# First attention slot leaves PSUM unscaled, and the loads of x for its mean square are spread over the passes

## The chip, the core and the metric

The kernel runs on one core of a Trainium2 chip. Its engines are TensorE (PE, with its weight loads shown apart as PEld), VectorE (DVE), ScalarE (ACT), GpSimd (POOL) and SyncE (SP, which here only issues DMAs). The metric is the device time of one execution in microseconds; lower is better.

## The reference, cut to what matters

One layer of an encoder with 256 tokens and width 2048, in float32:

```python
h = rms_norm(x, norm1_g)               # x * rsqrt(mean(x^2) + eps) * g
proj = h @ w_in                        # z | xBC | dt | q | k | v | GLU | gates
y_ssd = ssd_mixer(..., dt, ...) @ w_ssd_o
y_att = dilated_attention_mixer(q, k, v, q_g, k_g) @ w_attn_o
...
q = rms_norm(q.reshape(shape), q_g)    # per head, 128 wide
k = rms_norm(k.reshape(shape), k_g)
```

The factor `rsqrt(mean(x^2) + eps)` is one number for each token, called r below. Since it is a factor of the whole row, `h @ W` is `r * ((x * g) @ W)`. The kernel uses this for its first columns: it multiplies `x * g` with the weights of dt, q, k and v of the first head slot before r is known, and applies r to the results.

## The kernel before, in words

**Units.** All weights are streamed from HBM once. A weight block is a set of up to 512 output columns; it is cut into units of 256 rows of the weight (2 rows of 128 partitions). The main loop makes one pass for each unit, `for k in range(NU)`: it issues the weight load of unit k+5 on SP (five buffers `raw`), splits unit k+3 into a high and a low part (`split`: `hi` by ACT at L1211, `lo` by DVE at L255, four buffers each), issues the matmuls of unit k on PE (`mm`: L1273, L1274 and L1276 where activations are stationary, L1264, L1266 and L1268 where weights are), and then calls `S.tick`. So `hi` of unit k+3 can only be written when the matmuls of unit k-1 have read their `hi`, and `lo` when they have read their `lo`. "Unit k" and "pass k" below mean this number.

**Blocks at the start.** Units 0 to 7 are dt and q of slot 0 (448 columns), 8 to 15 k of slot 0 (384 columns), 16 to 23 v of slot 0 (384 columns). All three take `xgh`/`xgl`, the split of `x * g`. Units 24 to 31 are the first GLU block (512 columns); it and most later blocks take `hh`/`hl`, the split of the normed h. `job_h` makes these in four groups of four 128-row parts: four DVE products `hf` (L354), one ACT copy `hh` (L357), one DVE difference `hl` (L255, before the next group's `hl` but behind the next group's `hf` and `hh` in the code). Unit 24 needs group 0, unit 26 group 1, unit 28 group 2, unit 30 group 3. Two PSUM tiles `main` take turns, so block n+2 needs `main` of block n read.

**The planner.** What is to be done beside the stream is written as generators (jobs). A job yields requests: `("a", n)` or `("v", n)` asks to issue work that is costed at n ns on ACT or DVE, `"p"` on PE, `("m", n)` asks for n slabs of SBUF, `("b", n)` for banks of PSUM, `("w", n)` waits until n more passes have begun their tick, `("j", f)` waits until f is true. `S.tick` gives each engine credit: in a pass of 384 columns ACT gets (2600 - 950) * 0.75 * 0.95 = 1176 and DVE 1040, in a pass of 512 columns 1568 and 1387; credit left over is cut at 1.2 gains (1411 and 1248 for 384 columns). A request is granted while the credit is above zero, and may take it below zero. Jobs are asked in order of priority (0 first), then of age. All of this happens while the program is built: it sets the order in which each engine's instructions are issued.

**Forcing.** Before unit 24 is issued, `S.require` wants `hl` of group 0 to have been issued. If it isn't, it forces jobs without regard to credit or waits: first all jobs of priority 0 as far as they go, then those of priority 1 in order of age, until the condition is true. The same holds at units 26, 28 and 30.

**Jobs around the change.** `job_rms1` (priority 0, started in pass 3) loads x by four DMAs (`xr`, L318), squares it on ACT with a running sum (L325), makes r by ACT sqrt (L270) and five small DVE operations (`rstd_steps`, L273 to L283), stores it as `st["r1"]`, and calls `spread`: DVE makes a diagonal of r (`dg`, L291), PE multiplies it with ones (L296), and DVE copies the result to `rbc` (L338), which `job_h` (priority 1) waits for. `job_dt` (priority 1) multiplies dt's columns with r (L386) and permutes them on PE (L395). `job_qk` (priority 0) squares q or k from PSUM (L459), waits for r, makes the per-head factors by a second `rstd_steps`, multiplies them with r (L482), writes the normed `qn` from PSUM (L489), transposes it on PE (L501), and copies it out (L505, L506). `job_v` (priority 0) copies v out of PSUM times r (L517). `job_att` (priority 2) does the attention of the slot.

Of the kernel before, what the change touches and what calls it, by code (L numbers as in the profile page):

```python
# [15 lines left out]
AF = mybir.ActivationFunctionType  # L16
ALU = mybir.AluOpType
# [173 lines left out]
def kernel(ctx: ExitStack, tc: tile.TileContext, xT, xn, par, cm, cd, cq, w1, wq, ws, out):  # L191
    nc = tc.nc
    S = Sched()
# [11 lines left out]
    def nm(s):  # L205
        cnt[0] += 1
        return f"{s}_{cnt[0]}"

    def slab(shape, dt=F32, name="s"):
        return gp.tile([P] + list(shape), dt, tag="g", name=nm(name))  # L210

    def bank(shape=(512,), name="b"):
        return pd.tile([P] + list(shape), F32, tag="d", name=nm(name))

    def small(shape, name, dt=F32, bufs=None):
        return sm.tile([P] + list(shape), dt, tag=name, name=nm(name), bufs=bufs)

    V, A, G, PE = nc.vector, nc.scalar, nc.gpsimd, nc.tensor
# [11 lines left out]
    def par_(k, i=0, n=1):  # L230
        o = _OFF[k][0] + i
        return cpar[:, o:o + n]
# [11 lines left out]
    st = {}  # L244


    def natural(ap):

        return ap.rearrange("p (j r) -> p r j", r=2)

    def strided(ap):
        return ap.rearrange("p (r j) -> p r j", r=2)
# [29 lines left out]
            yield "v", 200 + n  # L282
        V.tensor_tensor(dst, r, s, op=ALU.mult)  # L283

    def spread(r):

        yield "m", 1
        dg = slab([2, P], name="dg")
        yield "v", 400
        for t in range(2):  # L290
            V.tensor_scalar(dg[:, t, :], ID, r[:, t:t + 1], None, op0=ALU.mult)  # L291
        yield "w", 1
        yield "b", 1
        b = bank()
        yield "p", 440
        PE.matmul(b[:, :T], ones, dg, start=True, stop=True)  # L296
        S.give()
        yield "w", 1
        return b[:, :T]
# [10 lines left out]
    def job_rms1():  # L310

        xss = small([2, 2], "xss1", bufs=1)
        yield "m", 4
        xs_ = []
        for t in range(2):
            for e in range(2):
                xr = slab([1024], name="xr")
                nc.sync.dma_start(xr, xn.rearrange("(p t) d -> p t d", t=2)[:, t, e * 1024:e * 1024 + 1024])  # L318
                xs_.append(xr)
        yield "w", 2  # L320
        for t in range(2):
            for e in range(2):
                yield "a", 1300
                xr = xs_[2 * t + e]
                A.activation(xr, xr, AF.Square, accum_out=xss[:, t, e:e + 1])  # L325
        S.give(4)
        yield "w", 1
        m2 = small([2], "ms2", bufs=2)
        yield "v", 300
        V.tensor_reduce(m2, xss, axis=AX.X, op=ALU.add)  # L330
        V.tensor_scalar(m2, m2, 1.0 / D, EPS, op0=ALU.mult, op1=ALU.add)
        r2 = cp.tile([P, 2], F32, name="r2")
        yield from rstd_steps(r2, m2, 2)
        st["r1"] = r2
        b = yield from spread(r2)
        rbc = small([T], "rbc", bufs=1)
        yield "v", 400
        V.tensor_copy(natural(rbc), strided(b))  # L338
        S.banks += 1
        st["rbc1"] = rbc  # L340
# [27 lines left out]
    def job_dt(main):  # L368
        bias = par_("dtb", 0, 64)
        yield "m", 2  # L370
        tmp = slab([8, P], name="dtt")
        pm_ = slab([2, T], name="perm")
        nc.scalar.dma_start(pm_, cq)
        dv, e, z, z2, q = (tmp[:, i, :] for i in range(5))
        raw = tmp[:, 5:7, :].rearrange("p a b -> p (a b)")
        dt = cp.tile([P, 2, 64], F32, name="dt")
        adt = cp.tile([P, 2, 64], F32, name="adt")
        adh = cp.tile([P, 2, 64], F32R, name="adh")
        adl = cp.tile([P, 2, 64], F32, name="adl")
        ea = cp.tile([P, 64], F32, name="ea")  # L380
        sp = cp.tile([P, 4, HEADS], F32, name="sp")
        st.update(dt=dt, adh=adh, adl=adl, sp=sp)
        yield "j", lambda: "r1" in st
        yield "v", 400
        for t in range(2):
            V.tensor_scalar(raw[:, 64 * t:64 * t + 64], main[:, t, 0:64], st["r1"][:, t:t + 1], None, op0=ALU.mult)  # L386
        V.memset(raw[:, P:P + 64], 0.0)
        st["dt_read"] = True
        yield "w", 1
        yield "b", 1  # L390
        ps = bank((2, P))
        yield "p", 900
        for t in range(2):
            for k in range(2):
                PE.matmul(ps[:, t, :], pm_[:, k, t * P:t * P + P], raw[:, 64 * k:64 * k + P],  # L395
                          start=(k == 0), stop=(k == 1))
        yield "w", 1
        yield "v", 300
        V.tensor_tensor(dv.rearrange("p (a b) -> p a b", a=2), ps[:, :, 0:64], bias[:, None, :].to_broadcast([P, 2, 64]),
                        op=ALU.add)  # L400
        S.banks += 1
        yield "a", 1900
        A.activation(e, dv, AF.Abs)
        A.activation(e, e, AF.Exp, scale=-1.0)
        A.activation(ea, par_("alog", 0, 64), AF.Exp)
        yield "w", 1
        yield "v", 1500
        V.tensor_scalar(z2, e, 2.0, None, op0=ALU.add)
        V.reciprocal(z, z2)
        V.tensor_tensor(z, z, e, op=ALU.mult)  # L410
        V.tensor_tensor(z2, z, z, op=ALU.mult)
        yield "v", 1000
        V.tensor_scalar(q, z2, 1.0 / 19.0, None, op0=ALU.mult)
        for n in (8, 7, 6, 5):
            V.scalar_tensor_tensor(q, q, 1.0 / (2 * n + 1), z2, op0=ALU.add, op1=ALU.mult)
        yield "v", 1000
        for n in (4, 3, 2, 1):
            V.scalar_tensor_tensor(q, q, 1.0 / (2 * n + 1), z2, op0=ALU.add, op1=ALU.mult)
        yield "v", 1000
        V.scalar_tensor_tensor(q, q, 1.0, z, op0=ALU.add, op1=ALU.mult)  # L420
        V.tensor_scalar(q, q, 2.0, None, op0=ALU.mult)
        V.scalar_tensor_tensor(dt.rearrange("p a b -> p (a b)"), dv, 0.0, q, op0=ALU.max, op1=ALU.add)
        for t in range(2):
            V.scalar_tensor_tensor(adt[:, t, :], dt[:, t, :], -1.0, ea, op0=ALU.mult, op1=ALU.mult)
        S.give(2)
        yield "w", 1
        yield "a", 200
        A.activation(adh, adt, AF.Copy)
        yield "w", 1
        yield "v", 200  # L430
        V.tensor_tensor(adl, adt, adh.bitcast(F32), op=ALU.subtract)
        yield "b", 1
        ps = bank((4, P))
        yield "p", 900
        for i, m in enumerate((GT, LE, LT, GE)):
            PE.matmul(ps[:, i, :], m, adt.rearrange("p a b -> p (a b)"), start=True, stop=True)
        yield "w", 1
        yield "a", 1500
        for i, o in enumerate((0, 64, 96, 32)):
            A.activation(sp[:, i, :], ps[:, i, o:o + HEADS], AF.Exp)  # L440
        S.banks += 1
        yield "w", 1
        yield "v", 300
        V.tensor_tensor(sp[:, 0, :], sp[:, 0, :], dt[:, 0, 0:32], op=ALU.mult)
        V.tensor_tensor(sp[:, 2, :], sp[:, 2, :], dt[:, 1, 32:64], op=ALU.mult)
        st["dt_done"] = True
# [3 lines left out]

    def job_qk(main, off, key, gain, scaled=False):

        yield "w", 1
        ss = small([6], "ss", bufs=3)
        junk = small([P], "junk", bufs=1)
# [7 lines left out]
        if scaled:  # L463
# [3 lines left out]
            r = st["r1"]  # L467
# [3 lines left out]
            for t in range(2):  # L471
                V.tensor_scalar(ms[:, t * 3:t * 3 + 3], ss[:, t * 3:t * 3 + 3], rr[:, t:t + 1], EPS,
                                op0=ALU.mult, op1=ALU.add)
# [12 lines left out]
        for t in range(2):  # L486
            for i in range(3):
                yield "a", 280
                A.activation(qn[:, t, i, :], main[:, t, off + i * P:off + i * P + P], AF.Copy,  # L489
                             scale=rs[:, t * 3 + i:t * 3 + i + 1])  # L490
        if off:
            yield "j", lambda: "dt_read" in st
        st["main_free"].add(id(main))
        st["q_blocks"] += 1
        yield "w", 3 if scaled else 1
        yield "b", 2
        bs = [bank((2, T)), bank((2, T))]
        yield "p", 650
# [11 lines left out]
    def job_v(main, j):  # L510
        yield "m", 1
        v = slab([2, 384], name="v")
        yield "j", lambda: j > 0 or "r1" in st
        yield "w", 1
        for t in range(2):
            yield "a", 450
            A.activation(v[:, t, :], main[:, t, 0:384], AF.Copy, scale=1.0 if j else st["r1"][:, t:t + 1])  # L517
        st["main_free"].add(id(main))
        st["q_blocks"] += 1
        qkv["v", j] = v  # L520


# [544 lines left out]
    def job_down(main, r, i):  # L1067
# [8 lines left out]
        for t in range(2):  # L1076
# [7 lines left out]
              main_free=set(), conv_t=set(), q_blocks=0, att_n=0, ssd_c=[0] * 4, ssd_n=0, z_n=0, z_g=[False] * 4, mg_n=0,  # L1084
# [16 lines left out]
    def start_jobs():  # L1101
        S.add(job_rms1(), "rms1", 0)
# [298 lines left out]
```

## Time and profile before

| | us |
|---|---|
| median of 3 runs (1982.23 to 1984.48) | 1983.19 |
| the profiled execution's own time | 1983.86 |
| its span, first to last instruction | 1982.1 |
| PE busy | 1966.0 (99%) |
| DVE busy | 1309.0 (66%) |
| ACT busy | 1036.0 (52%) |
| HBM read | 360.45 MB, 183 GB/s over the span |
| mean granted TensorE clock | 0.999 |

PE is busy nearly the whole span, and the chain that ended last is PE for 95% of it. So the profile is read by what is left: the few places where PE waits, and the one where its clock is low, are all in the first 100 us.

### The profile page before, as it was taken

The numbers are of one execution on the slowest core, as the hardware profiler recorded it, in microseconds if no ns is written. First come the engines' busy times: TensorE is split into PE (matmuls) and PEld (weight loads), VectorE is DVE, ScalarE is ACT, GpSimd is POOL, SyncE is SP. The second block draws the span as 40 slices with busy tenths as digits, with TensorE's granted clock in tenths as the row PEclk, the third lists the DMA queues.
The fourth block names the chain that finished last, engine by engine and source line by source line (L and its number), as shares of the span: only waits on it lengthen the run. The fifth ranks groups of instructions, "written<-read, shape, count | busy, mean of one in ns | idle before, by whom it ended". The sixth has DMA issues, their size and how long they took to land.

```text
span 1982.1 us, 29949 instructions
## 1 busy us (share of the span) xinstructions
PE 1966.0 (99%) x11798; PEld 1766.0 (89%) x11798; DVE 1309.0 (66%) x1847; ACT 1036.0 (52%) x1446; POOL 47.5 (2%) x42
## 2 busy tenths in 40 slices
PE   8999999999999999999999999999999999999999
PEld 7999999999998888888888888999988998998887
DVE  5778887887887889896654555555555554455443
ACT  6654576777757655545654444544443443344332
POOL 0000010000000000003000000000000000000000
PEclk9999999999999999999999999999999999999999
DMA  8555554554554555555555556555555555555554
GB/s 284 184 175 183 165 185 145 167 172 144 184 170 161 176 181 178 183 191 187 190 191 183 189 189 207 194 186 192 188 190 189 189 191 191 188 186 191 190 181 149
DMA packets 105342, 364.51 MB, mean 184 GB/s; under 512 B 11760, under 2 KB 12272, under 8 KB 105200
## 3 DMA queue, kind: packets, MB, share of 16 engines
q1 hardware_dynamic: 103904, 360.23, 55.4%
q10 hardware_dynamic: 1296, 2.36, 0.3%
q8 instruction: 92, 1.51, 0.3%
q14 instruction: 50, 0.41, 0.1%
HBM read 360.45 MB, written 2.10 MB: 183 GB/s over the span
## 4 chain that ended last, share of the span: by engine, by line
PE 95%; DVE 0%; issue 0%
PE main L1273 19%; PE main L1274 19%; PE main L1276 19%; PE main L1266 11%; PE main L1264 11%; PE main L1268 11%; PE b L842 1%; PE b L864 1%; PE b L968 1%; PE b L1273 0%; PE b L1274 0%; PE b L1276 0%; PE b L819 0%; PE b L501 0%; PE b L757 0%; PE b L742 0%
## 5 line engine op out<-in xcount | busy, mean ns | idle before, releaser
L255 DVE TENSOR_TENSOR lo<-raw,hi 128x1024 fp32r<-128x1024 f32 (+2 forms) x697 | 831.5, 1194 | 643.5 <-ACT hi L1211 638.7
L1211 ACT ACTIVATE hi<-raw 128x1024 fp32r<-128x1024 f32 (+2 forms) x695 | 716.2, 1032 | 868.7 <-PE main L1274 487.8
L1273 PE MATMUL main<-hi,hh 128*128 128x512 f32 (+1 forms) x800 | 306.1, 383 | 0.0
L1274 PE MATMUL main<-hi,hl 128*128 128x512 f32 (+1 forms) x800 | 299.0, 374 | 0.0
L1266 PE MATMUL main<-x2l,hi 128*128 128x256 f32 x1024 | 246.4, 281 | 0.0
L1264 PE MATMUL main<-x2h,hi 128*128 128x256 f32 x1024 | 246.3, 279 | 0.0
L1266 PE MATMUL main<-hl,hi 128*128 128x256 f32 x896 | 216.3, 281 | 3.2 <-DVE hl L255 3.2
L1264 PE MATMUL main<-hh,hi 128*128 128x256 f32 x896 | 217.7, 282 | 0.0
L565 DVE SCALAR_TENSOR_TENSOR co<-cin,cpar,co 128x256 f32<-128x256 f32 x480 | 211.1, 491 | 0.0
L1276 PE MATMUL main<-lo,hh 128*128 128x512 f32 (+1 forms) x800 | 200.5, 372 | 0.0
L1264 PEld LDWEIGHTS main<-x2h,hi 128*128 128x128 f32 x1024 | 192.7, 188 | 0.2
L1266 PEld LDWEIGHTS main<-x2l,hi 128*128 128x128 f32 x1024 | 192.6, 188 | 0.2
L1273 PE MATMUL main<-hi,ah 128*128 128x512 f32 x480 | 188.9, 394 | 0.0
L1274 PE MATMUL main<-hi,al 128*128 128x512 f32 x480 | 188.6, 393 | 0.0
L1273 PEld LDWEIGHTS main<-hi,hh 128*128 128x128 f32 x800 | 152.5, 191 | 23.4 <-ACT hi L1211 1.2
L1274 PEld LDWEIGHTS main<-hi,hl 128*128 128x128 f32 x800 | 152.2, 190 | 22.9 <-issue 1.9
L1266 PEld LDWEIGHTS main<-hl,hi 128*128 128x128 f32 x896 | 168.8, 188 | 4.2 <-DVE hl L255 3.6
L1264 PEld LDWEIGHTS main<-hh,hi 128*128 128x128 f32 x896 | 169.2, 189 | 0.6
L1276 PEld LDWEIGHTS main<-lo,hh 128*128 128x128 f32 x800 | 148.0, 190 | 22.1
L1268 PE MATMUL main<-x2h,lo 128*128 128x256 f32 x1024 | 138.3, 277 | 0.0
L1276 PE MATMUL main<-lo,ah 128*128 128x512 f32 x480 | 130.1, 393 | 0.0
L1268 PEld LDWEIGHTS main<-x2h,lo 128*128 128x128 f32 x1024 | 127.6, 188 | 0.0
(244 smaller groups left out, 2304.5 us busy)
## 6 DMA issues: line engine op xcount, KB each, us to landing
raw<-ws_dram SPq DMA_DIRECT2D x600, 512.0 KB, 3.3
raw<-wq_dram SPq DMA_DIRECT2D x88, 384.0 KB, 3.1
raw<-w_dram SPq DMA_DIRECT2D x7, 448.0 KB, 7.0
xr<-xn_dram SPq DMA_DIRECT2D x4, 512.0 KB, 9.2
x<-xn_dram SPq DMA_DIRECT2D x4, 512.0 KB, 4.3
xt<-xT_dram SPq DMA_DIRECT2D x7, 256.0 KB, 7.0
out_dram<-x SPq DMA_DIRECT2D x4, 256.0 KB, 3.7
out_dram<-x ACTq DMA_DIRECT2D x4, 256.0 KB, 5.6
```

Source lines behind the costliest of these rows:

```text
L255: V.tensor_tensor(lo, raw, hi.bitcast(F32), op=ALU.subtract)
L565: V.scalar_tensor_tensor(dst[:, e, :], x[:, e, k:k + T], par_("dw", (2 * i + e) * 31 + k), dst[:, e, :], op0=ALU.mult, op1=ALU.add)
L842: PE.matmul(ba, lt, src, start=(n == 0), stop=(n == 3))
L864: PE.matmul(bd[:, i, :], em[:, 0, i, :], x[:, c, pr:pr + P], start=True, stop=True)
L968: PE.transpose(b[:, e, t * P:t * P + P], src[:, t, k * P:k * P + P], ID)
L1211: A.activation(h, r, AF.Copy)
L1264: PE.matmul(o, wh[:, e, cs], ah, start=(first and e == 0 and c % 2 == 0), stop=False, skip_group_check=True)
L1266: PE.matmul(o, wh[:, e, cs], al, start=False, stop=False, skip_group_check=True)
L1268: PE.matmul(o, wl[:, e, cs], ah, start=False, stop=(last and e == 1), skip_group_check=True)
L1273: PE.matmul(o, ah[:, xs_], wh[:, e, :], start=(first and e == 0), stop=False)
L1274: PE.matmul(o, al[:, xs_], wh[:, e, :], start=False, stop=False)
L1276: PE.matmul(o, ah[:, xs_], wl[:, e, :], start=False, stop=(last and e == 1))
```

## The change

The four loads of `xr` are issued two passes apart instead of together. q, k and v of the first slot are copied from PSUM to SBUF as they are (`qraw`, and `v` in place), which frees `main` at once; r is applied to the copies. dt's columns are read from q's copy. `spread` waits two passes instead of one before its matmul, and q's and k's transposes come one pass after `qn` instead of three.

```diff
-    def spread(r):
+    def spread(r, wait=1):
...
-        yield "w", 1
+        yield "w", wait
         yield "b", 1
...
                 xr = slab([1024], name="xr")
                 nc.sync.dma_start(xr, xn.rearrange("(p t) d -> p t d", t=2)[:, t, e * 1024:e * 1024 + 1024])
                 xs_.append(xr)
-        yield "w", 2
+                yield "w", 2
+        yield "w", 1
...
-        b = yield from spread(r2)
+        b = yield from spread(r2, 2)
...
-        yield "j", lambda: "r1" in st
+        yield "j", lambda: "r1" in st and "dt_raw" in st
+        yield "w", 1
         yield "v", 400
         for t in range(2):
-            V.tensor_scalar(raw[:, 64 * t:64 * t + 64], main[:, t, 0:64], st["r1"][:, t:t + 1], None, op0=ALU.mult)
+            V.tensor_scalar(raw[:, 64 * t:64 * t + 64], st["dt_raw"][:, t, 0:64], st["r1"][:, t:t + 1], None, op0=ALU.mult)
...
     def job_qk(main, off, key, gain, scaled=False):
 
+        if scaled:
+            yield "m", 1
+            raw = slab([2, 448], name="qraw")
+            yield "w", 1
+            for t in range(2):
+                yield "a", 500
+                A.activation(raw[:, t, :off + 384], main[:, t, :off + 384], AF.Copy)
+            st["main_free"].add(id(main))
+            st["q_blocks"] += 1
+            main = raw
+            if off:
+                st["dt_raw"] = raw
...
-        if off:
-            yield "j", lambda: "dt_read" in st
-        st["main_free"].add(id(main))
-        st["q_blocks"] += 1
-        yield "w", 3 if scaled else 1
+        if scaled:
+            if off:
+                yield "j", lambda: "dt_read" in st
+            S.give()
+        else:
+            st["main_free"].add(id(main))
+            st["q_blocks"] += 1
+        yield "w", 1
...
-        yield "j", lambda: j > 0 or "r1" in st
         yield "w", 1
         for t in range(2):
             yield "a", 450
-            A.activation(v[:, t, :], main[:, t, 0:384], AF.Copy, scale=1.0 if j else st["r1"][:, t:t + 1])
+            A.activation(v[:, t, :], main[:, t, 0:384], AF.Copy)
         st["main_free"].add(id(main))
         st["q_blocks"] += 1
+        if j == 0:
+            yield "j", lambda: "r1" in st
+            yield "w", 1
+            for t in range(2):
+                yield "a", 450
+                A.activation(v[:, t, :], v[:, t, :], AF.Copy, scale=st["r1"][:, t:t + 1])
         qkv["v", j] = v
```

## The prediction

> **What bounds the kernel now.** First the page: span, and the chain that ended last.
>
> ```profile
> span 1982.1 us, 29949 instructions
> ...
> PE 95%; DVE 0%; issue 0%
> ```
>
> PE's own work sets the end, so a change can only win or lose where PE waits or runs at a lower clock. Second, PE's waits over the whole span, then four windows (us, PE busy, PEld, DVE, ACT, POOL busy, granted clock, DMA share, GB/s).
>
> ```profile
> PE b L296 <- DVE dg L291: 4.1, 1, 4.1
> PE main L1266 <- DVE hl L255: 3.2, 2, 2.2
> PE main L1273 <- ACT hi L1211: 2.9, 2, 2.1
> ```
>
> ```profile
> 37.00:41.20 4.20, 0.13 (x1) 0.00 (x0) 2.97 (x12) 2.77 (x6) 0.00 (x0) 1.00 0.69 189
> 41.20:44.80 3.60, 3.58 (x13) 3.40 (x14) 2.06 (x5) 2.46 (x11) 0.00 (x0) 0.53 0.59 176
> 44.80:73.00 28.20, 28.20 (x167) 27.93 (x167) 19.33 (x46) 20.04 (x46) 0.00 (x0) 1.00 0.57 182
> 73.00:101.00 28.00, 24.79 (x206) 24.28 (x205) 23.60 (x44) 13.00 (x17) 0.00 (x0) 1.00 0.54 173
> ```
>
> Three places matter: a wait of 2.1 us for `hi`, one of 4.1 for `dg` (with a clock of 0.53 for 3.6 us behind it), and 3.2 for `hl` in units 24 to 31, where DVE is busy 23.6 of 28 us. Third, PE in order of time at the first two.
>
> ```profile
> 28.31 0.34 PE L1273 MATMUL main<-hi,xgh 128*128 128x384 f32 x1
> ...
> 32.65 0.45 PE L1273 MATMUL main<-hi,xgh 128*128 128x384 f32 x1 [2.09 <-ACT hi L1211]
> ...
> 41.22 1.14 PE L296 MATMUL b<-dg,ones 128*128 128x256 f32 x2 [4.09 <-DVE dg L291]
> 42.16 1.91 PE L395 MATMUL b<-dtt,perm 128*128 128x128 f32 x8
> 43.73 0.67 PE L1273 MATMUL main<-hi,xgh 128*128 128x384 f32 x1
> ...
> 46.38 0.34 PE L1273 MATMUL main<-hi,xgh 128*128 128x384 f32 x1
> ...
> 48.46 0.34 PE L1273 MATMUL main<-hi,xgh 128*128 128x384 f32 x1
> ```
>
> These rows start units 8, 9, 11, 12 and 13; 12 to 13 gives an undisturbed unit, 2.09 us. Why unit 9 waits stands in the rows of SP and ACT.
>
> ```profile
> 16.20 4.69 SPq L318 DMA_DIRECT2D xr<-xn_dram  x4
> 21.57 34.26 SPq L1193 DMA_DIRECT2D raw<-wq_dram  x15
> ```
>
> ```profile
> 31.75 0.84 ACT L1211 ACTIVATE hi<-raw 128x768 fp32r<-128x768 f32 x1 [3.16 <-DMA raw<-wq_dram]
> ...
> 52.35 1.40 ACT L489 ACTIVATE qn<-main,qrs 128x128 f32<-128x128 f32 x5 [1.30 <-DVE qrs L482]
> ...
> 54.34 0.39 ACT L489 ACTIVATE qn<-main,qrs 128x128 f32<-128x128 f32 x1
> ...
> 60.15 0.21 ACT L270 ACTIVATE rs<-qms 128x6 f32<-128x6 f32 x1 [1.70 <-DVE qms L472]
> ...
> 67.20 1.10 ACT L357 ACTIVATE hh<-hf 128x1024 fp32r<-128x1024 f32 x1
> ...
> 73.97 0.67 ACT L505 ACTIVATE qkT<-b,cpar 128x512 f32<-128x512 f32 x1
> 74.53 0.46 ACT L506 ACTIVATE qkT<-b,cpar 128x256 f32<-128x256 f32 x1
> 74.89 1.05 ACT L517 ACTIVATE v<-main,r 128x384 f32<-128x384 f32 x2
> ```
>
> Four loads of x are issued ahead of unit 9's weights, which are issued at 21.57 and split only at 31.75.
>
> **The change, early part: a gain of 8.6 us.** Spread out, one load of x instead of four stands ahead of unit 9's weights; unit 9 then follows unit 8 directly. What it costs if not: the 2.1 us stay. The loads pass SP's queue one at a time between weight loads. r comes eight passes later, so L296 (two passes behind `dg`) moves behind unit 19, L395 behind unit 20 and q's transposes (one pass behind `qn`) behind unit 21, and nothing on PE waits for r before unit 24. Units 8 to 23 take 16 x 2.09 from 28.31, to 61.75. To this come L395, L296 and q's transposes at full clock:
>
> ```profile
> 106.87 0.89 PE b L436 x8
> ```
>
> This row of the chain has L395's shape and count in 0.89 us instead of 1.91, so I take 0.9 for L395 and 0.5 for L296 (1.14 by the same ratio). One set of transposes is 0.57 (72.32 to 72.89 below). Unit 23 ends at 63.7; with k's transposes the place where unit 24 could start is 64.3. Before, it started at 72.89: 8.6 us gained.
>
> The added ACT copies (448 wide out of PSUM, four) have no row; 384 wide out of PSUM took 0.53 (74.89, two in 1.05), 512 wide 0.67. I take 0.6 each; ACT's 8 us idle in the window 44.8 to 73.0 hide them. Without that cover they would cost 2.4 us.
>
> **The change, late part: h comes too late.** `job_h` starts from `rbc`, and ACT credit decides when it gets on. I worked the planner's ledger out by hand from the code. For the kernel before it gives five `qn` in pass 14 and one in pass 15, k's sqrt in pass 17 and `hh` of group 1 in pass 20: the ACT rows above show just that order. For the changed kernel (gain 1176, cap 1411):
>
> - pass 12: two squares of x at 1300, credit -1189; passes 14 and 15: one each, -263
> - pass 16: sqrt for r at 1502, -589; pass 17: r known, and k's two copies at 500, -414
> - pass 18: q's sqrt at 1506, -744; pass 19: two `qn` at 280, -128; pass 20: four more, -73, and `rbc` is issued
> - pass 21: five of k's squares at 260, -197 (DVE gets group 0's `hf` by now); pass 22: q's copies at 800 and k's last square, -82; pass 23: k's sqrt, -412
>
> `hh` of group 0 (950) never gets a turn, as every gain goes to priority 0. So at unit 24 the planner forces: first all that k and v still owe, then group 0's `hh`, group 1's `hf` and `hh`, and then `hl` of group 0. That chain stands in program order behind the split of unit 27, whose `lo` must wait for unit 23's end. Its prices:
>
> ```profile
> 50.27 0.18 DVE L273 RECIPROCAL rr<-rs 128x6 f32<-128x6 f32 x1
> ...
> 52.09 0.35 DVE L482 TENSOR_SCALAR qrs<-qrs,r 128x3 f32<-128x3 f32 x2
> ...
> 55.38 0.88 DVE L354 SCALAR_TENSOR_TENSOR hf<-xt,cpar,rbc 128x256 f32<-128x256 f32 x2
> ...
> 69.28 1.23 DVE L255 TENSOR_TENSOR lo<-raw,hi 128x1024 fp32r<-128x1024 f32 x1 [1.45 <-ACT hi L1211]
> 70.42 1.22 DVE L255 TENSOR_TENSOR hl<-hf,hh 128x1024 fp32r<-128x1024 f32 x1
> ```
>
> ```profile
> 72.32 0.82 PE L501 MATMUL b<-cmask,qn 128*128 128x128 f32 x6
> 72.89 0.37 PE L1264 MATMUL main<-hh,hi 128*128 128x256 f32 x1
> ...
> 94.43 1.11 PE L1268 MATMUL main<-hh,lo 128*128 128x256 f32 x8
> ...
> 100.09 1.12 PE L1268 MATMUL main<-hh,lo 128*128 128x256 f32 x8
> ```
>
> `lo` 26 waits for unit 22 (61.6) and ends at 63.0; four small DVE operations and k's sqrt, 64.0; `hi` 27, 65.0; `lo` 27, 66.2; five small operations (0.2 apart) and L482, 67.5; six `qn` (five in 1.40), 69.2; the last transpose, 69.5; L505 and L506, 70.6; four v copies of about 0.5 (two of them SBUF to SBUF, no row; between 0.28, a `qn`'s share, and 0.53), 72.6; `hh`, 73.7; `hl`, 74.9. With some 0.1 for hand-overs I take **75.5**. PE stands from 64.3 to 75.5, 11.2 us.
>
> The forcing leaves ACT's ledger near -6600 and DVE's near -3100. DVE's gain of 1387 for each pass doesn't bring it above zero by unit 26, so group 1 is forced there: `lo` 29 waits for unit 25's end (1.2), four `hf` (1.7), then `hl` (1.2), 4.2 us. The same at unit 28, 4.2 us, in which the slot's attention scores run on PE, as they do before; at unit 30 `lo` 33 and `hl`, 2.4. Units of this kind take (100.09 - 94.43) / 2 = 2.83. Unit 32 thus starts at 75.4 + 8 x 2.83 + 10.8 = 108.8; before, at about 100.09 + 0.95 = 101.05 (eight matmuls of L1268, 0.12 apart). That is **+7.8 us**, the early gain included.
>
> Then the clock. After 4.1 us without matmuls the clock was 0.53 for 3.6 us, which cost 3.6 x 0.47 = 1.7. The 11 us at unit 24 do this surely: +9.5. The 4.2 at unit 26 is as long as the gap that did it, yet barely; ends 0 and 1.7, and I take the middle: **+10.3**. The scores cut the gap at unit 28 to half.
>
> By the Trainium skill's page "TensorE: Matmul & The Clock Gate", Part 1, the clock falls to half after at least one idle window of about 3.4 us, and the window runs freely. By that rule the gap at unit 26 holds a whole window in about a quarter of the cases, and the sum would more often be +9.5 than +11.2. The trace agrees so far: 4.09 us idle, then 0.53.
>
> The profiled execution took 1983.86, 0.67 above the median. 1983.86 + 10.3 = 1994.2 for it, and 1993.5 against the median of 1983.19.
>
> **Rivals.** (1) *Faster: h gets its turn.* If `hh` of both groups, 1900 of ACT credit, were granted by pass 23, nothing is forced and the stage stays as before: 1983.2 - 8.6 = 1974.6. For it: ACT is idle some 30% of that window, and group 0's `hf` is done by about 59. Against it: the ledger is below zero at the end of each pass from 15 on, so it must be out by more than 1900. (2) *Half the stall.* Should k's remaining work be granted in time and only h be forced, the chain loses qn, transposes and copies, some 5 to 6 us: 1988. (3) *The debt goes on.* ACT's -6600 is four passes of gain; dt, attention and the first GLU read start late, and another forced wait or two of 2 to 4 us come after unit 32: 1996 to 2002. Against it: nothing waits there now, and main of units 24 to 31 need be read only by unit 40. (4) *The loads don't do what they are spread for:* 2.2 us more, 1995.7.
>
> **Chances.** A measurement of this kernel tells 0.2% (4 us: 1979.2 to 1987.2) from no change. Forecast, 1990 to 1997.5 with (4) in it: 0.66. (1) 0.11, (2) 0.12, half of it within 0.2%, (3) 0.11. So faster 0.11, same 0.06, slower 0.83. The range 1986 to 2001 leaves out (1), the lower end of (2) and the tail of (3), under 0.2.
>
> **What would show it.** Right: no wait at L296 and none at unit 9; unit 23 done near 64; behind it on ACT `qn`, `qkT`, four `v`, then `hh`, with PE waiting about 11 us for `hl` of L255 (split by the transposes), and again at units 26, 28 and 30; a clock near half behind it; from unit 32 no waits. Wrong: an `hh` on ACT before k's `qn`, or unit 24 starting below 66. Then the ledger is wrong, and rival (1) or (2) holds.

## The result, and the profile after

The changed kernel takes 2005.38 us (median of 4 runs, 2004.53 to 2006.41); beside it the kernel before took 1983.84 (4 runs, 1982.23 to 1985.33). The ratio is 1.0114, interval 1.0102 to 1.0126: slower by 21.5 us. The forecast was 1993.5, range 1986 to 2001. The sign held, and so did the early gain and the forced order behind unit 24; the size was half of what came, because the clock behind the shorter waits and the MLP were not priced.

The page of the changed kernel, span and chain that ended last:

```profile
span 2004.6 us, 29951 instructions
...
PE 94%; ACT 0%; DVE 0%; issue 0%
```

PE still sets the end, so 22.5 us of span must be PE waiting or PE running slower. PE's waits of the changed kernel over the whole span (total, times, longest, us) give the first half. Lines have moved: L1286, L1288 and L1290 are L1264, L1266 and L1268 of before; L1295 is L1273; `qn` is L503, the transposes L518, `hh` L358.

```profile
PE main L1288 <- DVE hl L255: 9.7, 4, 4.1
PE b L518 <- ACT qn L503: 5.9, 2, 5.5
PE main L1286 <- ACT hh L358: 3.4, 1, 3.4
PE main L1295 <- DVE cin L559: 1.9, 1, 1.9
```

The waits for `dg` (4.1) and for unit 9's `hi` (2.1) are gone. In their place stand 19.0 us (9.7, 5.9 and 3.4) for `hl`, `qn` and `hh`, and one wait for `cin` much later. ACT of the changed kernel in order of time shows why the first three come:

```profile
68.05 1.86 ACT L503 ACTIVATE qn<-qraw,qrs 128x128 f32<-128x128 f32 x6 [2.46 <-DVE qrs L496]
70.32 0.69 ACT L522 ACTIVATE qkT<-b,cpar 128x512 f32<-128x512 f32 x1 [0.41 <-PE b L518]
70.90 0.47 ACT L523 ACTIVATE qkT<-b,cpar 128x256 f32<-128x256 f32 x1
71.26 0.87 ACT L533 ACTIVATE v<-main 128x384 f32<-128x384 f32 x2
72.00 1.13 ACT L541 ACTIVATE v<-v,r 128x384 f32<-128x384 f32 x2
73.01 2.01 ACT L358 ACTIVATE hh<-hf 128x1024 fp32r<-128x1024 f32 x2
```

All that k and v owe goes ahead of `hh` of the first two groups: the planner's forced order at unit 24. PE of the changed kernel in order of time, from the last matmuls of unit 23 to unit 31:

```profile
62.18 0.86 PE L1298 MATMUL main<-lo,xgh 128*128 128x384 f32 x4
...
68.50 0.48 PE L518 MATMUL b<-cmask,qn 128*128 128x128 f32 x1 [5.46 <-ACT qn L503]
...
74.13 0.58 PE L1286 MATMUL main<-hh,hi 128*128 128x256 f32 x1 [3.43 <-ACT hh L358]
...
75.39 0.58 PE L1288 MATMUL main<-hl,hi 128*128 128x256 f32 x1 [0.68 <-DVE hl L255]
...
78.56 1.11 PE L1290 MATMUL main<-hh,lo 128*128 128x256 f32 x8
...
86.68 0.58 PE L1288 MATMUL main<-hl,hi 128*128 128x256 f32 x1 [4.07 <-DVE hl L255]
...
90.05 1.91 PE L1290 MATMUL main<-hh,lo 128*128 128x256 f32 x8
...
99.03 0.58 PE L1288 MATMUL main<-hl,hi 128*128 128x256 f32 x1 [2.29 <-DVE hl L255]
...
102.31 1.11 PE L1290 MATMUL main<-hh,lo 128*128 128x256 f32 x8
...
108.98 0.58 PE L1288 MATMUL main<-hl,hi 128*128 128x256 f32 x1 [2.62 <-DVE hl L255]
...
112.35 1.16 PE L1290 MATMUL main<-hh,lo 128*128 128x256 f32 x8
```

PE is held at units 24, 26, 28 and 30. Behind each wait the time from the first L1288 to L1290 is 3.17, 3.37, 3.28 and 3.37 us; in unit 31, which follows no wait, it is 1.78. Windows of the changed kernel (us, PE, PEld, DVE, ACT, POOL busy, granted clock, DMA share, GB/s) show what goes with it; the granted clock is the share of TensorE's full speed that it was given:

```profile
75.30:78.50 3.20, 3.11 (x15) 3.11 (x16) 0.04 (x1) 0.00 (x0) 0.00 (x0) 0.53 0.02 5
82.40:86.60 4.20, 0.21 (x2) 0.00 (x1) 3.93 (x6) 1.30 (x2) 0.00 (x0) 0.82 0.67 237
86.60:90.00 3.40, 3.32 (x15) 3.33 (x16) 0.02 (x1) 0.00 (x0) 0.00 (x0) 0.50 0.00 1
96.70:99.00 2.30, 0.04 (x1) 0.00 (x0) 2.28 (x4) 1.06 (x1) 0.00 (x0) 0.95 0.67 226
99.00:102.30 3.30, 3.27 (x15) 3.27 (x16) 0.00 (x0) 0.00 (x0) 0.00 (x0) 0.52 0.00 1
106.40:108.90 2.50, 0.00 (x0) 0.00 (x0) 2.33 (x2) 0.14 (x1) 0.00 (x0) 1.00 0.59 184
108.90:112.30 3.40, 3.32 (x15) 3.32 (x16) 0.03 (x1) 0.00 (x0) 0.00 (x0) 0.52 0.39 143
```

After every one of the four waits the clock is about half for some 3.3 us. Together that is 13.2 - 4 x 1.78 = 6.1 us, and 0.8 for the slow L1290 of unit 26 (1.91 instead of 1.11): **6.9 us**.

Where the time is lost is read from the distance between the start of the same unit in the two profiles (worked out from PE's rows in order of time):

| place (time in the profile before, us) | after minus before, us |
|---|---|
| unit 5 (21.0) | -1.0 |
| unit 23 (70.2) | -9.4 |
| unit 31 (98.2) | +15.2 |
| middle of the first projection (158 to 164) | +14.9 |
| start of the MLP (1264) | +17.0 |
| last units (1969) | +22.0 |

The first 1.0 is the start of these two executions, before the change does anything. So the change wins 8.4 up to unit 23, loses 24.6 in units 24 to 31, 1.9 to 2 more by the MLP, and **5.0 in the MLP, where PE waits for nothing**. There the up-projection takes the split of the second norm, `x2h` and `x2l`, in units of 24 matmuls of 256 columns. One window of 44 us in its first stretch, before and after:

```profile
1310.00:1354.00 44.00, 44.00 (x381) 44.00 (x380) 24.27 (x22) 20.25 (x20) 0.00 (x0) 1.00 0.58 192
```

```profile
1327.00:1371.00 44.00, 44.00 (x374) 44.00 (x373) 23.25 (x22) 20.76 (x20) 0.00 (x0) 1.00 0.54 184
```

PE is busy in both throughout and the clock is full, yet 374 matmuls get done where 381 did. The MLP has four such stretches of 32 units. The first holds some work of other jobs, the other three take 90.83 us each after and 89.39 before (means; the figures per 32 units below are of the same three). Over all four the changed kernel loses 5.6 us. The down-projection between them takes 88.4 to 88.8 us per 32 units in both, and 0.6 comes back in its last stretch.

### The profile page after: what moved, and what is told of

Read it like the earlier page. It is cut to its first block, busy times and chain, and to the rows that moved or that the text cites. A ratio compares the mean times of both kernels' runs of the same rounds, so it can differ in the third digit from the quotient of the medians.

```text
span 2004.6 us, 29951 instructions
## 1 busy us (share of the span) xinstructions
PE 1975.9 (99%) x11798; PEld 1776.0 (89%) x11798; DVE 1310.6 (65%) x1847; ACT 1043.5 (52%) x1454; POOL 42.8 (2%) x42
## 4 chain that ended last, share of the span: by engine, by line
PE 94%; ACT 0%; DVE 0%; issue 0%
PE main L1295 19%; PE main L1296 19%; PE main L1298 19%; PE main L1286 11%; PE main L1288 11%; PE main L1290 11%; PE b L886 1%; PE b L864 1%; PE b L990 1%; PE b L1295 0%; PE b L1296 0%; PE b L1298 0%; PE b L841 0%; PE b L518 0%; PE b L779 0%; PE b L764 0%
## 5 line engine op out<-in xcount | busy, mean ns | idle before, releaser
L1295 PE MATMUL main<-hi,hh 128*128 128x512 f32 (+1 forms) x800 | 304.7, 381 | 1.9 <-DVE cin L559 1.9
L1286 PE MATMUL main<-x2h,hi 128*128 128x256 f32 x1024 | 248.1, 281 | 0.0
L1288 PE MATMUL main<-x2l,hi 128*128 128x256 f32 x1024 | 247.7, 281 | 0.0
L1288 PE MATMUL main<-hl,hi 128*128 128x256 f32 x896 | 221.4, 284 | 9.7 <-DVE hl L255 9.7
L1286 PE MATMUL main<-hh,hi 128*128 128x256 f32 x896 | 222.7, 287 | 3.4 <-ACT hh L358 3.4
L1286 PEld LDWEIGHTS main<-x2h,hi 128*128 128x128 f32 x1024 | 194.2, 190 | 0.2
L1288 PEld LDWEIGHTS main<-x2l,hi 128*128 128x128 f32 x1024 | 193.4, 189 | 0.2
L1295 PE MATMUL main<-hi,ah 128*128 128x512 f32 x480 | 188.6, 393 | 0.0
L1288 PEld LDWEIGHTS main<-hl,hi 128*128 128x128 f32 x896 | 172.9, 193 | 11.2 <-DVE hl L255 10.6
L1286 PEld LDWEIGHTS main<-hh,hi 128*128 128x128 f32 x896 | 172.7, 193 | 4.4 <-ACT hh L358 3.8
L1295 PEld LDWEIGHTS main<-hi,hh 128*128 128x128 f32 x800 | 152.3, 190 | 24.8 <-DVE cin L559 2.4
L1290 PE MATMUL main<-x2h,lo 128*128 128x256 f32 x1024 | 142.2, 282 | 0.0
L1290 PEld LDWEIGHTS main<-x2h,lo 128*128 128x128 f32 x1024 | 130.3, 190 | 0.0
```

What stands on the lines that cost most here:

```text
L1286: PE.matmul(o, wh[:, e, cs], ah, start=(first and e == 0 and c % 2 == 0), stop=False, skip_group_check=True)
L1288: PE.matmul(o, wh[:, e, cs], al, start=False, stop=False, skip_group_check=True)
L1290: PE.matmul(o, wl[:, e, cs], ah, start=False, stop=(last and e == 1), skip_group_check=True)
L1295: PE.matmul(o, ah[:, xs_], wh[:, e, :], start=(first and e == 0), stop=False)
```

## The experiments

Theory: the planner's order makes h late (units 24 to 31), the waits cool the clock, and the MLP's loss is the place of `x2h` and `x2l` in SBUF, which the change shifts. Rivals: the copies or the loads cost by themselves; the clock has nothing to do with it; the MLP's loss is the delay itself, or DMA. Every time below is a median, and every ratio is against the kernel before, run on the same chip. Line numbers shift by a few from kernel to kernel; the tiles of a row tell which instruction it is.

### Ask h before the rest

```diff
-    S.add(job_h(), "h", 1)
+    S.add(job_h(), "h", 0)
```

> The changed kernel with one edit: the job that makes h has priority 0 instead of 1, so it is asked before k's norm. If the planner's order is the cause (the ledger of ACT credit never lets h have its turn, and unit 24 forces everything at once), the waits for hh and hl at units 24, 26, 28 and 30 go, the early gain stays, and the time is 1972 to 1982. If the lateness of r itself is the cause (r comes eight passes later, whatever is asked first), PE still waits 8 us or more at unit 24 and the time stays above 1995.

1978.07 us (8 runs), ratio 0.9975 (0.9965 to 0.9986). PE's waits of this kernel:

```profile
PE main L1288 <- DVE hl L255: 5.2, 2, 4.0
PE main L1295 <- DVE cin L559: 1.9, 1, 1.9
```

The 19.0 us are down to 5.2, nothing is forced at units 24 to 30, and the kernel is 27.3 us faster than the changed one. At unit 31 it is 24.1 us ahead of it (23.6 on a common start); the MLP, where it loses 1.5 us to the kernel before instead of 5.1 (89.5 us per 32 units), adds 3.6 more. Copies and spread loads are still in it, so neither by itself makes units 24 to 31 slow: the order does. This version beats both kernels, the one before by 0.25%. The wait of 4.0 at unit 24 is left (low clock behind it), because group 0's `hl` still comes behind group 1's `hf` and `hh` in the code.

### The copies without the spread loads

```diff
                 xs_.append(xr)
-                yield "w", 2
-        yield "w", 1
+        yield "w", 2
```

> The changed kernel with the four loads of x issued together again, as before; the copies out of PSUM, spread's two passes and the rest of the change stay. If the spread loads make r, and so h, too late, this one has r about seven passes earlier: the 2 us wait at unit 9 is back, the 4 us wait for dg and the low clock behind it stay gone, h comes in time, and the time is 1974 to 1984. If the copies and the added requests of ACT credit are what makes h late, unit 24 still waits several us and the time is 1990 or more.

1982.51 us (10 runs), ratio 0.9996 (0.9987 to 1.0005). The time is that of before, but not for the reason expected. PE's waits of this kernel:

```profile
PE main L1287 <- DVE hl L255: 9.7, 3, 6.4
PE main L1294 <- ACT hi L1232: 2.5, 2, 1.5
PE b L296 <- DVE dg L291: 2.0, 1, 2.0
```

The `dg` wait is halved; the waits for `hl` are tripled (9.7 against 3.2), at units 24, 26 and 28, of which the planner forces 26 and 28. So h comes somewhat late even when r comes early. The copies' ACT credit would do that, and so would `spread`'s second pass, which this kernel keeps; no run parts the two. At unit 31 the kernel is 5.0 us behind before. It wins 3.7 back up to unit 199, where PE waits for nothing, and 2.7 in the MLP (88.9 us per 32 units). The time of before is thus the sum of a loss and two gains, and that it fell into the expected range is luck.

### The spread loads without the copies

```diff
                 xs_.append(xr)
-        yield "w", 2
+                yield "w", 2
+        yield "w", 1
```

> The kernel before with one part of the change: the four loads of x issued two passes apart. Main of q is then still read times r, so unit 16 needs r, which the planner has not asked for by then: it forces the whole chain from the squares of x to qn before unit 16. Expected by the theory that the planner's forcing sets the price: the 2 us at unit 9 go, but PE waits 15 us or more before unit 16, and the time is 1995 to 2015. If the loads alone were harmless: 1976 to 1982.

The edit is on the kernel before. 2010.73 us (4 runs), ratio 1.0139 (1.0122 to 1.0156). PE's waits of this kernel:

```profile
PE b L396 <- issue: 10.0, 1, 10.0
PE b L502 <- ACT qn L490: 9.2, 2, 8.9
PE b L437 <- DVE adt L425: 8.6, 1, 8.6
PE b L296 <- DVE dg L291: 3.3, 1, 3.3
```

With r late and dt and q still in `main`, the planner forces at unit 16, which needs that tile read, and PE waits some 31 us in four places. The copies do what they are for: in the changed kernel these waits are absent. The late r costs in either kernel; it only comes due at another place.

### Keep the clock up through the waits

```diff
+        def turnover(n):
+            b = bank()
+            for _ in range(n):
+                PE.matmul(b[:, 0:P], ones, ones, start=True, stop=True)
...
+        if k == 24:
+            turnover(22)
...
+        if k in (24, 26, 28, 30):
+            turnover({24: 13, 26: 16, 28: 9, 30: 10}[k])
```

> The changed kernel with matmuls of ones into a spare PSUM bank put where PE waits: before the forced work of unit 24 and ahead of units 24, 26, 28 and 30, each set a little shorter than its wait. Nothing reads them. If the low clock behind those waits is a cost of its own, beside the waits, the granted clock stays near 1 there and about 5 us of the 6.5 that these units lose to it come back: 1999 to 2002. If the clock is only a companion of the waits, the time stays at 2004.5 to 2006.5, and if the added matmuls delay the transposes it grows.

Matmuls that nobody reads fill the changed kernel's waits. 1999.26 us (4 runs), ratio 1.0084 (1.0068 to 1.0099): 6.1 us less than the changed kernel. Windows of this kernel around unit 26:

```profile
82.40:86.70 4.30, 3.81 (x35) 3.61 (x33) 3.95 (x6) 1.22 (x2) 0.00 (x0) 1.00 0.61 227
86.70:91.00 4.30, 4.30 (x37) 4.30 (x38) 1.23 (x1) 1.06 (x1) 0.00 (x0) 1.00 0.00 2
```

PE is busy through most of the wait and the clock stays at 1.00 behind it, where it was 0.50. The same holds at units 28 and 30. At unit 24 two gaps of 0.66 and 0.87 us are left, and the clock is 0.50 from 76.17 to 79.58. The distance from before at unit 31 falls from 15.2 to 9.8 us, so 5.4 us come back; the sum above has 5.5 for units 26, 28 and 30. By test the low clock behind these three is thus worth 5.4 us at unit 31, and 6.1 of the 21.5 in the medians. The MLP is that of the changed kernel to 0.01 us in every unit: `x2h` and `x2l` lie where they lie there, and the earlier start changes nothing. The delay is not what slows the MLP.

### Move the MLP's operand alone

```diff
+        if i == 0:
+            pads = [slab([2, 512], name="pad") for _ in range(2)]
+            for pad in pads:
+                V.memset(pad[:, 0, 0:1], 0.0)
+            V.tensor_tensor(pads[0][:, 0, 0:1], pads[0][:, 0, 0:1], pads[1][:, 0, 0:1], op=ALU.add)
```

> The kernel before; when the first x2 tile is made, two more slabs are taken and a single column of each is written, so that the four x2h and four x2l tiles land in other slabs of SBUF. The order of everything else stays. If PE's rate in the MLP units that stream x2h and x2l depends on where these lie, the units of the up projection take another time than 2.79 us, alike in all sixteen of their blocks, and the kernel's time moves by 1 to 6 us either way, with the down projection near where it was and the first 1250 us untouched. If the 5 us that the changed kernel loses there come from something else, the up units stay within 0.01 us of before and the time at 1983.5.

The edit is on the kernel before: two slabs of SBUF are taken where the first `x2h` is made, so that the eight tiles fall into other slabs. 1987.46 us (10 runs), ratio 1.0021 (1.0012 to 1.0030). In the traces the start of its units against before stays at -2.4 us from unit 16 to the start of the MLP, and is +1.7 at the end (1.9 of the -2.4 is the start of the two executions): 4.1 us are lost, all of them in the MLP. A window of this kernel at the same place of the MLP:

```profile
1310.40:1354.40 44.00, 44.00 (x376) 44.00 (x376) 23.05 (x22) 20.76 (x20) 0.00 (x0) 1.00 0.56 186
```

376 matmuls in 44 us, against 381 before and 374 after; 90.4 us per 32 units. The down-projection takes what it takes before, to 0.2 us. Nothing of the change is in this kernel, so the place alone makes some 4 us.

### More of the same: nearer loads, and other places

Three kernels vary the loads and h's priority, and three more move the MLP's tiles.

```diff
-                yield "w", 2
-        yield "w", 1
+                yield "w", 1
```

On the changed kernel (loads one pass apart, so r some five passes earlier):

> The changed kernel with one edit: the loads of x one pass apart instead of two, r five passes earlier. By the planner's ledger, h still does not get its turn: units 24, 26 and 28 are forced, with k's and v's rest before group 0 at unit 24, but less of k is owed and unit 30 is not forced. If the forcing sets the price, the time lies between copies_only and the changed kernel: 1985 to 2002. If two passes between the loads were what matters by itself, it falls to 1980 or below.

2000.08 us (4 runs), ratio 1.0088 (1.0074 to 1.0102). PE's waits of this kernel:

```profile
PE main L1287 <- DVE hl L255: 11.2, 3, 4.3
PE b L517 <- ACT qn L502: 3.9, 2, 2.5
PE main L1294 <- DVE cin L558: 1.9, 1, 1.9
```

The time is inside the expected range. With r earlier the stall shrinks from 19.0 to 15.1 us, but units 24, 26 and 28 are still forced: even so the loads are not close enough for h at priority 1.

The same edit with h at priority 0:

> The changed kernel with h asked first (priority 0), and the four loads of x issued one pass apart instead of two, so that r comes five passes earlier. By the planner's order nothing is forced. If the forcing and the lateness of r are all that costs, the 4.0 us wait for hl that h_first still has at unit 24, with the low clock behind it, goes, the wait of 1.9 us for cin goes too, and the early gain of 8 to 9 us stays: 1970 to 1977. If close loads bring back the wait at unit 9, 1976 to 1980.

1983.22 us (11 runs), ratio 1.0002 (0.9993 to 1.0011): a miss. PE's waits of this kernel:

```profile
PE b L517 <- ACT qn L502: 3.0, 2, 2.6
PE main L1294 <- ACT hi L1229: 1.9, 1, 1.9
```

Waits are the fewest of all kernels here, and at the MLP's start it is 6.3 us ahead of before. Then the MLP takes 6.1 us of it back: 90.9 us per 32 units. The expectation had left the place out.

Loads together with h at priority 0 (`yield "w", 2` once, behind the loop):

> The changed kernel with h asked first and the four loads issued together, as before. Nothing is forced by the planner's order. The wait of 2 us at unit 9 is expected back, the rest as in h_first_close: 1973 to 1980, some 2 us above h_first_close but for the placement of tiles. If the spread loads had a use beyond unit 9 (an earlier landing elsewhere), the difference is over 4 us.

1987.89 us (7 runs), ratio 1.0023 (1.0013 to 1.0034): a miss on the other side. The waits for `hi` at units 9 on are back (3.7), and it is 1.2 us behind before at the MLP's start and 5.7 at the end (2.6 and 7.1 on a common start; 90.6 per 32 units). The difference to the kernel above was to be 2 us but for the place and came out as 4.7, although the MLP takes less here (4.6 us lost against 6.1). By the expectation's own words, over 4 means that the spread loads have a use beyond unit 9. At the MLP's start the two kernels are 8.7 us apart on a common start; PE's waits make up 5.8 of that, for `hi` and `dg` above all, and the rest is open.

Two of the three that move tiles start from h at priority 0 with loads one pass apart. The first takes six slabs at the first `x2h` (as above, `range(6)`), the second two at every `x2h` (`if True`):

> h_first_close with six more slabs at that place. h_first_close is 6.3 us ahead of the kernel before at unit 430 and loses 6 of it in the MLP, where its up units take 2.84 us. By the placement theory this version keeps the 6.3 us up to there and then loses or wins with its own placement: 1974 to 1985, 1977 at the middle placement seen (2.79 us). If h_first_close lost the 6 us otherwise, 1983 again.

> h_first_close with two more slabs at each of the four x2 tiles: a third placement. The same expectation as for close_pads_a, with another time for the up units: 1974 to 1985. Of the two, the one with the shorter up units is to be the faster one, by 128 times the difference.

1979.69 us (11 runs), ratio 0.9981 (0.9972 to 0.9990), and 1981.03 (11 runs), 0.9988 (0.9979 to 0.9997), with 90.3 and 90.6 us per 32 units. Both are inside the expected range, and the one with the shorter up units is faster by 1.3 us, as expected. Against the kernel with h at priority 0 and loads one pass apart (1983.22), the edit that touches nothing but the place takes off 3.5 us. The last takes five slabs in the changed kernel:

> The changed kernel, with five more slabs taken when the first x2 tile is made, so that x2h and x2l lie elsewhere in SBUF. Everything up to unit 430 is the same. If the 5 us that the changed kernel loses in the MLP come from where these tiles lie, its up units (2.84 us on average) take another time, alike in all blocks, and the kernel's time moves with them by 1 to 8 us (2.72 to 2.88 us were seen in the runs so far), while the lag at unit 430 stays at 17 us. If they come from the change itself, up units and time stay within 0.01 us and 1 us.

2006.92 us (4 runs), ratio 1.0117 (1.0103 to 1.0130): a miss. The sum of the units hardly changed (90.78 against 90.83 per 32), which is what the expectation had for a loss that is not the place's. But which units are slow did change. The eight units of a block read the four `x2h` and the four `x2l` tiles in pairs: the first two units the first of each, the next two the second, and so on. A unit of each pair takes:

| kernel | first pair, us | second | third | fourth |
|---|---|---|---|---|
| before | 2.79 | 2.81 | 2.77 | 2.81 |
| changed | 2.83 | 2.87 | 2.83 | 2.83 |
| changed, tiles moved | 2.88 | 2.83 | 2.83 | 2.81 |

In all thirteen kernels the two units of a pair agree to 0.04 us, and pairs of one kernel differ by up to 0.11. So the time goes with the tiles that a unit reads, and the slow pair moves when the tiles do. Which places are fast isn't known.

## Why the prediction failed

**Early part: right.** No wait at L296, none at unit 9; unit 23 is 8.4 us earlier, against 8.6 forecast.

**The forced order at unit 24: right.** The ledger gave the order `qn`, transposes, `qkT`, four v copies, `hh`, `hl`, and the rows of ACT show it. The first L1288 was forecast at 75.5 and stands at 75.39. With the profile's start 1.0 us early, that is 0.9 more on the common start: unit 23's end to that matmul is 12.4 us, less 0.57 of transposes 11.8, against 11.2. The wait at 26 was 4.07 (forecast 4.2), at 30 2.62 (2.4), at 28 2.29 behind the 1.9 us of the attention scores (together 4.2, forecast 4.2). Forced waits were forecast as the effect of priority and credit, and the run with h at priority 0 shows that: without the forcing, unit 31 starts 23.6 us earlier on a common start.

**"Then the clock": the first step that failed, a term too small.** The prediction charged 1.7 for the stall at unit 24 "surely", half of 1.7 at unit 26, and nothing at 28 and 30: 2.55 us. All four waits were followed by about half clock, at 1.4 to 1.6 us up to L1290 and 2.4 in all at unit 26, 6.9 in sum, 4.3 more than charged. The run with filler matmuls shows it as cause: 5.4 us at unit 31 come back, where the rows of units 26, 28 and 30 have 5.5. The error was to take the one gap of before (4.09 us idle) as the shortest that does it, and the rule of the Trainium skill's page "TensorE: Matmul & The Clock Gate", Part 1 (half after at least one idle window of about 3.4 us) as support. By that rule units 28 and 30, after 2.29 and 2.62 us, would run at full clock. They ran at 0.52, so here the measurement decides against it; how much idle time is enough stands in the last section. On the common start unit 31 is 16.1 us late, close to the forecast's +10.3 for unit 32 plus 4.3 for the clock and 0.9 for the stall; some 0.6 is unassigned.

**"The debt goes on", a rival at 0.11: partly right.** A wait of 1.92 us for `cin` stands at 588 us, in pass 200, where the planner of the changed kernel forces block 23's reading. It is found in just the five kernels here whose planner forces there, and no run tests it alone. Around it the distance from before is not still: it falls by 1.5 us from unit 31 to 199, rises by 2.2 at the wait and by 1.1 from there to the MLP. The 1.9 us put down to `cin` below is the sum of all three.

**The MLP: the second step that failed, not in the sum at all.** The prediction ended at unit 32 ("from unit 32 no waits") and took equal work for equal time, without giving a reason. In the MLP there are no waits, yet 5.0 us came from PE's own rate. The pads run shows that place alone makes 4 us; the run with fillers excludes the delay; that DMA did it has no support (its share in the windows is lower after, 0.54, than before, 0.58). That the changed kernel's 5.0 are its own slabs' is inferred, since the one run that moved them moved the slow units and not the sum.

The terms beside each other: clock +4.3, MLP +5.0, unit 32 to the MLP with `cin` +1.9, the stall +0.9, unassigned +0.6, start -1.0: 11.7 us; measured less forecast is 11.9 (2005.38 - 1993.5). The range missed because it held one of these terms, the clock, only in part and the MLP not at all.

## What to carry to other kernels

When a planner grants work by credit and priority, making one product late (here r) shifts who is forced at the next deadline; give the job with the nearest deadline the first turn. Where PE is the bound, price a wait at its own length and, from some 2 us on, at the half clock that may follow it; here that was 1.4 to 2.4 us for each of four waits, and filler matmuls in the waits won most of it back. After any change of what is allocated when, compare PE's rate in a stretch without waits before laying a few us to the edit itself.

## What the runs showed of the hardware that was not expected

**A short wait halves the clock when enough of it falls into one cell of a fixed grid of 3.41 us.** In the changed kernel, waits of 2.29 and 2.62 us were followed by half clock. In the run with the copies alone a wait of 2.49 us was not, and in the kernel before one of 2.17 us was not. So the length doesn't decide alone. Within each of the thirteen traces the granted clock changes only at times that lie a multiple of 3.41 us apart; in the changed kernel it does so at 68.06, 78.30, 85.13, 91.96, 98.78, 102.20, 109.02 and 112.44. Cut along this grid, the changed kernel's cells around units 28 and 30 (the second figure is PE's busy time) are:

```profile
95.37:98.78 3.41, 1.37 (x11) 1.12 (x9) 3.41 (x6) 0.90 (x1) 0.00 (x0) 1.00 0.61 217
98.78:102.20 3.42, 3.17 (x15) 3.17 (x16) 0.20 (x1) 0.15 (x1) 0.00 (x0) 0.50 0.05 18
102.20:105.61 3.41, 3.41 (x30) 3.41 (x30) 1.23 (x1) 3.02 (x6) 0.00 (x0) 1.00 0.02 5
105.61:109.02 3.41, 0.79 (x8) 0.59 (x6) 2.36 (x2) 0.93 (x1) 0.00 (x0) 1.00 0.60 167
109.02:112.44 3.42, 3.42 (x16) 3.42 (x17) 0.00 (x0) 0.00 (x0) 0.00 (x0) 0.50 0.37 140
```

The cells of the run with the copies alone, around its wait of 2.49, and then those of the kernel before, around its wait of 2.17:

```profile
88.00:91.41 3.41, 2.48 (x21) 2.28 (x20) 2.80 (x6) 1.95 (x2) 0.00 (x0) 1.00 0.49 154
91.41:94.83 3.42, 1.86 (x15) 1.86 (x16) 1.51 (x2) 0.06 (x1) 0.00 (x0) 1.00 0.46 153
94.83:98.24 3.41, 3.41 (x28) 3.31 (x27) 2.12 (x2) 1.06 (x1) 0.00 (x0) 1.00 0.02 5
```

```profile
85.70:89.12 3.42, 1.86 (x13) 1.55 (x12) 3.32 (x7) 1.07 (x2) 0.00 (x0) 1.00 0.47 163
89.12:92.53 3.41, 2.80 (x23) 2.80 (x24) 1.69 (x2) 0.68 (x1) 0.00 (x0) 1.00 0.48 156
```

In the changed kernel PE is idle for 2.04 and 2.62 us of one cell, and the next cell runs at half clock. In the other two the wait is cut in two by the grid: 0.93 and 1.56 us, 1.56 and 0.61 us, and the clock stays. The same count over all thirteen traces, from the first full clock to 8 us before the end: 24 cells at full clock in which PE was idle for 1.90 us or more were all followed by half clock; of twelve with 1.5 to 1.9 us, two were; of those with less, none. Full clock came back after the first cell with at most 0.5 us idle. The Trainium skill's page "TensorE: Matmul & The Clock Gate", Part 1, has the window run freely, and the grid of 3.41 us agrees with that; no run here moves a wait against the grid on purpose.

**PE's rate depends on where its moving operand lies in SBUF.** Over the thirteen kernels, whose matmuls in the MLP are the same, one up-projection unit of 24 matmuls of 256 columns takes 2.72 to 2.88 us, and 32 of them 88.9 to 90.9, at a clock of 1.00 and with PE busy throughout. Where nothing is moved, the time repeats: with fillers the changed kernel's MLP units start 5.4 us earlier and take the same to 0.01 us. A rule that names the fast slabs was not found.
